# All of p @ w_ple beside the last tile's routing, the last two down products by column halves, and a final gate that begins on the first halves

## The chip, the cores and the metric

One core of a Trainium2 chip runs the whole program. PE is the tensor engine, DVE the vector engine, ACT the scalar engine, POOL and SP mainly issue DMAs here. The metric is the device time of one execution in microseconds; lower is better.

## The reference

One layer on 1024 tokens (rows) of 1024 columns, in float32. After attention and a gated linear mixer the layer ends so:

```python
    h = h + merged @ w_out[l]
    h = h + expert_choice_ffn(rmsnorm(h, norm_ffn[l]), w_router[l],
                              w_exp_gate[l], w_exp_up[l], w_exp_down[l])
    ple_gate = jax.nn.sigmoid(rmsnorm(h, norm_ple[l]) @ w_ple_gate[l])
    h = h + ple_gate * (p[l] @ w_ple[l])
return rmsnorm(h, norm_final)
```

`expert_choice_ffn` has 16 experts. Each takes the 128 tokens with the largest affinity to it, computes `silu(x @ gate) * (x @ up) @ down` with three weights of 1024x1024, scales by the affinity and adds the result to those tokens' rows of h. p has 1024 rows of 256 columns, `w_ple` is 256x1024.

## The kernel before

Rows are worked in eight tiles of 128. To keep float32 precision every product is made of three matmuls (`mm3`): both operands are split into a high part, rounded by ACT (L131, L828, L851), and the rest, which DVE makes (`split`, `parts`, `mpiece`). A product of a tile with a 1024x512 block is thus 24 matmuls of 512 columns.

The part up to h = h + merged @ w_out is followed by the routing. For each tile PE multiplies by `w_out` (`w_half`), DVE adds the old h, ACT and PE make logits (`h_turned`, `router`, `affinities`, `aff_turned`), and DVE sorts the affinities of all tiles (`one_tile` and others). When the last tile (7) is sorted, a threshold per expert is spread by two small transposes of `cg`, ranks come from matmuls with `tri` and `ones`, and `tokens(0)` and `gather(0)` fetch the first expert's rows. Half of p @ w_ple (rows 0 to 511) lies beside this: p is turned on PE (`p_turned`) after tile 5 and multiplied in eight half products of six matmuls (`p_half`), which ACT scales into a buffer `pw` that is stored to the DRAM tensor `pw_d` after each four.

The expert loop runs gate and up of expert e, then down of expert e-1. Weights come in pieces of 1 MB through a ring of 15 buffers (`cycle`) from several pools (wraw, rawA to rawE, rawX), which also hold other things before and after the loop. `hidden_turned` transposes the product of gate and up. Each down product is scaled on ACT into `y` and added to h in DRAM (`h_d`) by an indirect DMA that POOL issues (the scatter).

After the loop the second half of p is loaded, turned and multiplied, the weight `w_pg` (`w_ple_gate`) is loaded and split with its gain, h is read back, and `front(t)` and `ple(t)` make the final gate: transposes of h, a sum of squares (`junk`, ACT), 48 matmuls, then tanh, product with p's rows, sums and the last norm.

While `in_order` is set PE keeps the order of the code; before, it is unset after the last down product. Elsewhere a scheduler orders each engine, and an engine works its queue strictly in order. PSUM has eight banks of 512 columns, in four pairs `mm`, `b`, `tr` (transposes) and `a`.

Of the kernel before, what the change touches and what calls it, by code (L numbers as in the profile page):

```python
# [9 lines left out]
F32 = mybir.dt.float32  # L10
# [11 lines left out]
NT = 8  # L22
D = 1024
KC = 8
# [43 lines left out]
def tile_hybrid_block(  # L68
# [57 lines left out]
    def turn(*args):  # L126
        return on_pe(nc.tensor.transpose(*args))  # L127
# [1003 lines left out]
        elif t == 6:  # L1131
            merged(top[0:NE], one_tile(6), slice(0, NE), top)

    placed = None
    in_order[0] = True
    for t in range(NT):
        was = [{}, {}]
        if t:
            was = [{3: partial(h_turned, t - 1), 6: partial(router, t - 1)},
                   {1: partial(affinities, t - 1), (3 if t > 5 else 7): partial(aff_turned, t - 1)}]  # L1140
        for c in range(2):
            w_half(t, c, was[c])

        if t == 2:
            p_raw = p_load(slot(rawX, (2, 4, 256))[:, 0], 0)
            wp = parts(loaded(rawX, (2, D), w_ple), (2, D), (rawC, rawC))
        if t == 5:
            pT = slot(rawC, (2, 4, 2, 128), F32R)
            p_turned(p_raw, pT)


    def p_half(n):
        nonlocal pw
        i, c = n // 2, n % 2
        if n % 4 == 0:
            pw = slot(rawX, (2, D))
        p_product(pw, pT, wp, i, (c,))
# [5 lines left out]
    for f, more in ((h_turned, (1,)), (router, (2,)), (affinities, (3, 4)), (aff_turned, (5, 6, 7))):  # L1163
        f(NT - 1)
        for n in more:
            p_half(n)
    last = one_tile(NT - 1)
    sO.close()
    eg = ctx.enter_context(pool("eg", bufs=2))
# [8 lines left out]
    pt = bank("a")  # L1178
    for i in range(2):
        turn(pt[:, i * NE:(i + 1) * NE], cg[:, i:i + 1].to_broadcast([NE, 128]), ident[0:NE, 0:NE])  # L1180
    thr = o1.tile([128, 2, NE], F32, name="thr")
    nc.vector.tensor_copy(thr, pt[:, 0:2 * NE].rearrange("p (i e) -> p i e", i=2))

# [24 lines left out]
    def tokens(e):  # L1208
        oh = eg.tile([128, NT, 128], BF16, name="oh", bufs=1)
        nc.vector.tensor_tensor(oh, posT[:, :, e:e + 1].to_broadcast([128, NT, 128]),  # L1210
                                iot.unsqueeze(1).to_broadcast([128, NT, 128]), op=ALU.is_equal)
        pi = bank("a")
        for t in range(NT):
            nc.tensor.matmul(pi[:, 0:2], oh[:, t], tok[:, t], start=t == 0, stop=t == NT - 1)  # L1214
# [10 lines left out]

    found = tokens(0)
    gathered = gather(0)

    so1.close()


# [69 lines left out]
    def up(e, after):  # L1301
# [6 lines left out]
        for c in range(2):  # L1308
            cc = slice(c * 512, c * 512 + 512)
            nc.vector.scalar_tensor_tensor(s["hid"][:, cc], pu[c], s["col"][:, NE:NE + 1], s["hid"][:, cc],  # L1310
                                           op0=ALU.mult, op1=ALU.mult)

    def hidden_turned(e):
        st[e]["hT"] = hl_pair(e2, "hT")
        for g in range(2):
            turned(st[e]["hid"], *st[e]["hT"], g, "tr")

# [29 lines left out]

    begin(0)
    for e in range(NE):
        last = {1: partial(hidden_turned, e)} if e == NE - 1 else {}  # L1350
        gate(e, {1: partial(hidden_turned, e - 1)} if e else {0: first_tokens})
        up(e, {1: partial(tokens_of, e + 2)} if e else {2: partial(ahead, 1)})
        if e:
            down(e - 1, {0: partial(ahead, e + 1), **last})
    down(NE - 1, {})

    in_order[0] = False


    def next_slot(shape, dt=F32):  # L1360
        return slot(next_pool(), shape, dt)

    cycle, n_pieces = [rawC] * 4 + [rawX] * 2 + [wraw] * 2 + [rawE] * 2 + [rawB] * 2 + [rawD], [0]
    pws = {}
    p_raw = p_load(next_slot((2, 4, 256))[:, 0], 4)
    wp = parts(loaded(next_pool(), (2, D), w_ple), (2, D), (next_pool(), next_pool()))
    pT = next_slot((2, 4, 2, 128), F32R)
    p_turned(p_raw, pT)
    wg = {(k, 0): mpiece(w_pg, 4 * k, 0, next_pool(), LL, gain=plcol) for k in range(2)}
    for i in range(4):  # L1370
        if i % 2 == 0:
            pw = next_slot((2, D))
        p_product(pw, pT, wp, i)
        pws[4 + i] = pw[:, i % 2]
    sE.close()
    f2 = ctx.enter_context(pool("f2", bufs=2, side="right"))
    hs_ = {}

    def rows(src, t, n=2):

        r = next_pool().tile([128, 2, D], F32, tag="raw", name="raw")
        return r, nc.sync.dma_start(r[:, 0:n], src[t * 128:(t + n) * 128].rearrange("(c p) n -> p c n", p=128)).ins

    def keep(d, t, n, r):
        d.update({t + i: r[:, i] for i in range(n)})

    r, first = rows(h_d, 0, 1)
    keep(hs_, 0, 1, r)
    with tc.issue_after(first):
        wg.update({(k, 1): mpiece(w_pg, 4 * k, 512, next_pool(), AA, gain=plcol) for k in range(2)})  # L1390
        keep(pws, 0, 2, rows(pw_d, 0)[0])
        keep(hs_, 1, 2, rows(h_d, 1)[0])
        nfin = next_pool().tile([128, 2, D], F32, tag="raw", name="raw")[:, 0]
        nc.sync.dma_start(nfin, bcast_row(norm_final, D))
        for t in (2, 4, 6):
            keep(hs_, t + 1, 2 if t < 6 else 1, rows(h_d, t + 1, 2 if t < 6 else 1)[0])
            if t == 2:
                keep(pws, t, 2, rows(pw_d, t)[0])
    F = {}

    def transposed(src, th, tl, g):

        pt = bank("tr")
        for c in range(4):
            turn(pt[:, c * 128:(c + 1) * 128],
                                src[:, (g * 4 + c) * 128:(g * 4 + c + 1) * 128], ident)
        split(th[:, g * 4:g * 4 + 4], tl[:, g * 4:g * 4 + 4], pt.rearrange("p (c t) -> p c t", c=4))

    def front(t):
        ht = hs_[t]  # L1410
        nT = hl_pair(f2, "nT")
        for g in range(2):
            transposed(ht, *nT, g)
# [6 lines left out]
        F[t] = ht, nT, rh  # L1420

    def ple(t):
        tt = slice(t * 128, (t + 1) * 128)
        ht, nT, rh = F[t]
        pw = pws[t]
        last = t == NT - 1
        groups = [(0, 512), (512, 256), (768, 256)] if last else [(0, 512), (512, 512)]
        ss = small.tile([128, 3], F32, name="ss3")
        for i, (c0, n) in enumerate(groups):
            po = bank("mm")  # L1430
            for k in range(KC):
                w = wg[k // 4, c0 // 512]
                ws = slice(c0 % 512, c0 % 512 + n)
                mm3(po[:, 0:n], nT[0][:, k], nT[1][:, k], w[0][:, k % 4, ws], w[1][:, k % 4, ws], k == 0, k == KC - 1)
# [7 lines left out]
        nc.vector.tensor_reduce(sm, ss[:, 0:len(groups)], axis=X, op=ALU.add)  # L1442
        rs = rstd_of(sm, D)
        for c in range(2):
            cc = slice(c * 512, c * 512 + 512)
            nc.vector.scalar_tensor_tensor(ht[:, cc], ht[:, cc], rs, nfin[:, cc], op0=ALU.mult, op1=ALU.mult)
            (nc.sync if last else nc.gpsimd).dma_start(out[tt, cc], ht[:, cc])

    front(0)
    front(1)  # L1450
    for t in range(NT):
        if t + 2 < NT:
            front(t + 2)
        ple(t)


# [29 lines left out]
```

## Time and profile before

| | |
|---|---|
| three runs | 1714.88, 1716.77, 1717.15 us; median 1716.77 |
| profiled execution: own time | 1719.85 us |
| its span in the profile | 1718.1 us |
| PE busy | 1649.0 us, 96% of the span |
| DVE, ACT busy | 1175.6 us, 903.4 us |
| mean granted PE clock | 0.985 of full speed |

The span is the time from the first to the last record; the execution's own time holds 1.75 us around it. Times in the text count from the start of the span.

### The profile page before, as it was taken

The numbers are of one execution on the slowest core, as the hardware profiler recorded it, in microseconds if no ns is written. First come the engines' busy times: TensorE is split into PE (matmuls) and PEld (weight loads), VectorE is DVE, ScalarE is ACT, GpSimd is POOL, SyncE is SP. The second block draws the span as 40 slices with busy tenths as digits, with TensorE's granted clock in tenths as the row PEclk, the third lists the DMA queues.
The fourth block names the chain that finished last, engine by engine and source line by source line (L and its number), as shares of the span: only waits on it lengthen the run. The fifth ranks groups of instructions, "written<-read, shape, count | busy, mean of one in ns | idle before, by whom it ended". The sixth has DMA issues, their size and how long they took to land. (4 is left out here: it accounts for less than half of the span.)

```text
span 1718.1 us, 23091 instructions
## 1 busy us (share of the span) xinstructions
PE 1649.0 (96%) x8795; PEld 1356.6 (79%) x8795; DVE 1175.6 (68%) x2228; ACT 903.4 (53%) x1265; POOL 155.8 (9%) x186
## 2 busy tenths in 40 slices
PE   6998999999999999999999869999999999999897
PEld 6977766667989898988887647888888887777786
DVE  7546755543474747463356878999999998888566
ACT  4235555441453535352033237777777777777632
POOL 1013300000000000000001110111111111100010
PEclk9999999999999999999999979999999999999999
DMA  6032302325112121126452589999999999992711
GB/s 233 2 106 103 130 26 62 112 85 184 50 55 69 44 80 39 49 74 226 153 197 112 189 328 383 383 395 388 392 397 390 396 387 368 377 379 90 269 50 49
DMA packets 123607, 335.06 MB, mean 195 GB/s; under 512 B 9180, under 2 KB 41988, under 8 KB 123496
## 3 DMA queue, kind: packets, MB, share of 16 engines
q1 hardware_dynamic: 106784, 277.96, 44.2%
q0 software_dynamic: 14704, 53.17, 9.1%
q10 hardware_dynamic: 2008, 2.46, 0.4%
q8 instruction: 69, 1.13, 0.3%
q14 instruction: 42, 0.34, 0.1%
HBM read 290.50 MB, written 43.06 MB: 194 GB/s over the span
## 5 line engine op out<-in xcount | busy, mean ns | idle before, releaser
L131 DVE TENSOR_TENSOR slot<-slot 128x2048 fp32r<-128x2048 f32 (+1 forms) x200 | 446.4, 2245 | 52.7 <-ACT slot L131 50.2
L131 ACT CAST slot<-slot 128x2048 fp32r<-128x2048 f32 (+1 forms) x200 | 374.8, 1879 | 103.9 <-PE ps_mm L124 56.7
L124 PE MATMUL ps_mm<-aT_h,wh 128*128 128x512 f32 x512 | 203.0, 397 | 1.2 <-ACT sgr L273 1.2
L124 PE MATMUL ps_mm<-aT_h,wl 128*128 128x512 f32 x512 | 204.1, 399 | 0.0
L124 PE MATMUL ps_mm<-aT_l,wh 128*128 128x512 f32 x512 | 203.8, 398 | 0.0
L124 PE MATMUL ps_mm<-slot,xt_h 128*128 128x512 f32 x512 | 161.6, 396 | 3.1 <-DVE slot L131 2.7
L124 PE MATMUL ps_b<-slot,xt_h 128*128 128x512 f32 x512 | 160.2, 393 | 4.0 <-DVE slot L131 4.0
L124 PE MATMUL ps_mm<-slot 128*128 128x512 f32 x576 | 142.1, 401 | 0.0
L124 PEld LDWEIGHTS ps_mm<-slot 128*128 128x128 f32 x576 | 108.1, 192 | 24.7 <-issue 1.4
L124 PEld LDWEIGHTS ps_b<-slot,xt_h 128*128 128x128 f32 x512 | 95.1, 188 | 24.8 <-DVE slot L131 5.7
L124 PEld LDWEIGHTS ps_mm<-slot,xt_h 128*128 128x128 f32 x512 | 95.7, 190 | 23.8 <-DVE slot L131 3.5
L124 PEld LDWEIGHTS ps_mm<-aT_h,wh 128*128 128x128 f32 x512 | 97.2, 190 | 18.7 <-ACT sgr L273 1.4
L124 PEld LDWEIGHTS ps_mm<-aT_h,wl 128*128 128x128 f32 x512 | 97.5, 190 | 18.3 <-issue 1.2
L124 PEld LDWEIGHTS ps_mm<-aT_l,wh 128*128 128x128 f32 x512 | 97.1, 190 | 18.3 <-issue 1.2
L131 DVE TENSOR_TENSOR wl<-raw,wh 128x2048 fp32r<-128x2048 f32 (+1 forms) x29 | 61.5, 2121 | 64.1 <-ACT wh L131 64.1
L124 PE MATMUL ps_mm<-slot,xt_l 128*128 128x512 f32 x256 | 100.4, 392 | 0.6 <-DVE xt_l L131 0.6
L131 ACT CAST wh<-raw 128x2048 fp32r<-128x2048 f32 (+1 forms) x30 | 52.1, 1735 | 92.0 <-PE ps_mm L124 87.3
L124 PE MATMUL ps_b<-slot,xt_l 128*128 128x512 f32 x256 | 99.8, 390 | 0.0
L124 PE MATMUL ps_mm<-wh,aT_l 128*128 128x256 f32 x320 | 89.4, 280 | 1.8 <-DVE aT_l L131 1.8
L124 PE MATMUL ps_mm<-wh,aT_h 128*128 128x256 f32 x320 | 90.7, 283 | 0.4 <-DVE sgr L615 0.4
L124 PE MATMUL ps_mm<-wl,aT_h 128*128 128x256 f32 x320 | 89.6, 280 | 0.0
L124 PE MATMUL ps_mm<-slot,nT_h 128*128 128x512 f32 (+1 forms) x272 | 81.8, 381 | 0.3 <-ACT nT_h L131 0.3
(381 smaller groups left out, 3311.4 us busy)
## 6 DMA issues: line engine op xcount, KB each, us to landing
slot<-in_w_exp_gate_dram SPq DMA_DIRECT2D x64, 1024.0 KB, 7.9
slot<-in_w_exp_down_dram SPq DMA_DIRECT2D x64, 1024.0 KB, 8.3
slot<-in_w_exp_up_dram SPq DMA_DIRECT2D x60, 1024.0 KB, 7.7
raw<-in_w_in_dram SPq DMA_DIRECT2D x16, 1024.0 KB, 6.6
raw<-in_w_in_dram SPq DMA_DIRECT2D x14, 512.0 KB, 5.2
sg_d<-sgr POOLq DMA_DIRECT2D x14, 512.0 KB, 3.0
xn_d<-xa POOLq DMA_DIRECT2D x8, 520.5 KB, 3.8
xt<-in_x_dram SPq DMA_DIRECT2D x8, 512.0 KB, 6.7
```

What stands on the lines that cost most here:

```text
L124: return on_pe(nc.tensor.matmul(*args, **kw))
L131: return nc.scalar.copy(hi, src), eng.tensor_sub(lo, src, hi)
```

## The change

1. p is loaded whole after tile 2 and turned in two parts, after tiles 4 and 5. Half products 8 to 11 stand after the first eight, 12 behind the transposes of `cg`, 13 and 14 behind the rank matmuls, 15 behind `gather(0)`. The search of the first expert's tokens takes its place in PE's fixed order. Nothing of p is left after the expert loop but the reading of `pw_d`.
2. The down products of experts 14 and 15 go in column halves, in the order 14 first half, 15 first half, 14 second half, 15 second half, each with a scatter of 128x512 into h seen as 2048 rows of 512. Expert 15's hidden rows are turned behind the first piece.
3. The first halves of rows 0 to 255 of h are read between the second and the third scatter, and turned inside and behind the last half product. The gate's first 4 of 8 blocks of k of tiles 0 and 1 (48 matmuls) stand ahead of everything that needs the second halves. PE's order stays fixed to the end.

```diff
@@ -1142,11 +1142,13 @@
         if t == 2:
-            p_raw = p_load(slot(rawX, (2, 4, 256))[:, 0], 0)
+            p_raw = slot(rawX, (2, 4, 256))
+            for i in range(2):
+                p_load(p_raw[:, i], 4 * i)
...
-        if t == 5:
-            pT = slot(rawC, (2, 4, 2, 128), F32R)
-            p_turned(p_raw, pT)
+        if t in (4, 5):
+            pTs.append(slot(rawC, (2, 4, 2, 128), F32R))
+            p_turned(p_raw[:, t - 4], pTs[-1])
...
+    for n in range(8, 12):
+        p_half(n)
     last = one_tile(NT - 1)
...
+    p_half(12)
...
+    p_half(13)
+    p_half(14)
...
     gathered = gather(0)
-
+    p_half(15)
     so1.close()
...
+    def down_half(e, c, po, after=()):
+
+        s = st[e]
+        cc = slice(c * 512, c * 512 + 512)
+        for k2 in range(2):
+            n = n_pieces[0]
+            raw = loaded(next_pool(), (4, 512), w_ed[e][k2 * 512:k2 * 512 + 512, cc])
+            hi, lo = [slot(rawE if n % 3 == 2 else whl, (4, 512), F32R) for _ in range(2)]
+            split(hi, lo, raw)
+            for k in range(4):
+                kk = 4 * k2 + k
+                mm3(po, s["hT"][0][:, kk], s["hT"][1][:, kk], hi[:, k], lo[:, k], kk == 0, kk == KC - 1)
+            for f in after if k2 == 0 else ():
+                f()
+        nc.scalar.mul(s["y"][:, cc], po, s["col"][:, e:e + 1])
+        nc.gpsimd.indirect_dma_start(out=h_d[:, :].rearrange("t (c n) -> (t c) n", c=2), in_=s["y"][:, cc],
+                                     in_offset=None, compute_op=ALU.add,
+                                     out_offset=bass.IndirectOffsetOnAxis(ap=idx2[:, e % 2, c:c + 1], axis=0))
...
-    down(NE - 1, {})
-
-    in_order[0] = False
...
+    down_half(e0, 0, po[0], (partial(hidden_turned, e1), first_rows))
+    down_half(e1, 0, po[2])
+    r01 = rows(rawD, h_d, 0, LO, queue=nc.gpsimd)
+    hs_.update({0: r01[:, 0], 1: r01[:, 1]})
+    cycle = [rawX] * 2 + [wraw] * 2
+    down_half(e0, 1, po[1])
...
+    down_half(e1, 1, po[3], (partial(first_turn, 0),))
+    first_turn(1)
...
+    begun = {}
+    for t in range(2):
+        begun[t] = [bank("b" if t else "mm") for _ in range(2)]
+        for po, (c0, n) in zip(begun[t], columns(t)):
+            product(po, t, c0, n, range(4))
     front(0)
     front(1)
```

How instructions move. On PE in the routing, before (-) and after (+); `affA` is the transpose of tile 7's affinities, `cg` the threshold, `tri` the rank matmuls:

```order
-L124 MATMUL ps_b<-slot 128x512 x18
+L124 MATMUL ps_b<-slot 128x512 x42
 L127 MATMUL ps_a<-ident,cg 128x16 x2
+L124 MATMUL ps_b<-slot 128x512 x6
 L124 LDWEIGHTS tri
 L124 MATMUL ps_a<-msk,tri 128x256
```

24 matmuls of p now stand between the affinities and the threshold, six between it and the ranks.

On POOL at the end of the expert loop, after the change (L1335 is the scatter of a half, from y for expert 14 and from a buffer named hid for 15, L1392 the read of h, DMASW and DMAHW are DMA semaphores):

```order
L1335 DMA h_d<-y,idx_14170 2048x512 [waits DMASW6_49,Activation_49]
L1335 DMA h_d<-hid,idx_14170 2048x512 [waits DMASW7_49,DVE_49,Activation_49]
L1392 DMA raw<-h_d 128x2x512 [waits DMAHW3_49,DMAHW4_49,DMAHW2_49,DMAHW5_49,DMAHW1_49,DMAHW6_49,DMAHW0_49,DMAHW7_49,DMASW0_49,DVE_49]
L1335 DMA h_d<-y,idx_14170 2048x512 [waits DMASW1_49,Activation_49]
L1335 DMA h_d<-hid,idx_14170 2048x512 [waits DMASW2_49,Activation_49]
```

Where there were two scatters of whole rows there are four of half rows and a read between them, and each waits for the DMA ahead of it.

On PE and then on ACT, after the change, where the gate's first halves end (`ps_b<-slot x24` is tile 1's part of them; the transposes are those of the second halves of tiles 0 and 1, then both halves of tile 2):

```order
L124 MATMUL ps_b<-slot 128x512 x24
L127 MATMUL ps_tr<-ident,raw 128x128 [waits DMAHW5_49,PE_49]
L127 MATMUL ps_tr<-ident,raw 128x128 x3
L127 MATMUL ps_tr<-ident,raw 128x128 [waits PE_49]
L127 MATMUL ps_tr<-ident,raw 128x128 x3
L127 MATMUL ps_tr<-ident,raw 128x128 [waits DMAHW6_49,DVE_49]
L127 MATMUL ps_tr<-ident,raw 128x128 x3
L127 MATMUL ps_tr<-ident,raw 128x128 [waits DVE_49]
L127 MATMUL ps_tr<-ident,raw 128x128 x3
L124 MATMUL ps_mm<-slot 128x512 [waits Activation_49]
```

```order
L1457 ACTIVATE junk,ssf<-raw 128x1024 [waits DMAHW5_49,DMASW1_49]
L1457 ACTIVATE junk,ssf<-raw 128x1024 [waits Activation_49]
L1457 ACTIVATE junk,ssf<-raw 128x1024 [waits DMAHW6_49,Activation_49]
L1457 ACTIVATE junk,ssf<-raw 128x1024 [waits DVE_49,Activation_49]
L131 CAST slot<-ps_tr 128x512 [waits PE_49] x2
L131 CAST nT_h<-ps_tr 128x512 [waits PE_49] x2
```

ACT's queue has the sums of squares of tiles 0 to 3 ahead of the casts of the second halves, and the third of them waits for the same load (DMAHW6) as PE's transposes of tile 2.

## Rows read from the trace of the kernel before

**Rows 1.** The page, part 1: busy us, share of the span, instructions.
```profile
PE 1649.0 (96%) x8795; PEld 1356.6 (79%) x8795; DVE 1175.6 (68%) x2228; ACT 903.4 (53%) x1265; POOL 155.8 (9%) x186
```

**Rows 2.** Windows of 20 us: length, PE, PEld, DVE, ACT, POOL busy, PEclk, DMA, GB/s.
```profile
1000.00:1020.00 20.00, 6.01 (x43) 4.57 (x41) 14.87 (x57) 7.67 (x9) 4.08 (x4) 0.69 0.76 294
...
1600.00:1620.00 20.00, 16.05 (x62) 12.30 (x61) 11.79 (x27) 15.04 (x26) 0.00 (x0) 0.83 0.89 331
```

**Rows 3.** The chain that ended last, in order of time, within the final gate.
```profile
1642.17 10.69 PE ps_mm L124 x47
```

**Rows 4.** Timeline of PE, tail: start, us, engine line op out<-in xcount [idle before <-releaser].
```profile
1569.23 0.61 PE L124 MATMUL ps_mm<-slot,hT_h 128*128 128x512 f32 x2
...
1594.19 1.03 PE L127 MATMUL ps_tr<-ident,slot 128*128 128x128 f32 x8
...
1606.12 6.96 PE L124 MATMUL ps_b<-slot 128*128 128x512 f32 x18 [3.33 <-ACT slot L1042]
...
1614.30 0.73 PE L124 MATMUL ps_mm<-slot,nT_h 128*128 128x512 f32 x2 [0.34 <-ACT nT_h L131]
...
1640.87 0.64 PE L127 MATMUL ps_tr<-ident,raw 128*128 128x128 f32 x4
...
1708.79 0.28 PE L124 MATMUL ps_mm<-slot,nT_l 128*128 128x256 f32 x1
```

**Rows 5.** A window of 1 us inside the wait for p's products.
```profile
1605.00:1606.00 1.00, 0.00 (x0) 0.00 (x0) 1.00 (x3) 1.00 (x3) 0.00 (x0) 0.50 0.85 319
```

**Rows 6.** Timeline of POOL and SP: the last scatter, the first read of h.
```profile
1595.35 1.54 POOL L1328 DMA_INDIRECT h_d<-y,idxs  x1 [9.85 <-ACT y L1327]
...
1601.63 0.34 SPq L1382 DMA_DIRECT2D raw<-h_d  x1
```

**Rows 7.** DMA issues, single ones and groups: KB each, median us to landing.
```profile
h_d<-y,idxs POOLq DMA_INDIRECT x1, 9.5
h_d<-y,idxs POOLq DMA_INDIRECT x1, 6.1
raw<-h_d SPq DMA_DIRECT2D x1, 512.0 KB, 3.6
h_d<-ht POOLq DMA_DIRECT2D x8, 512.0 KB, 2.9
xg<-xn_d,idxs POOLq DMA_INDIRECT x1, 6.2
xg<-xn_d,idxs POOLq DMA_INDIRECT x16, 8.7
```

**Rows 8.** Timeline of ACT and DVE in the tail.
```profile
1593.70 1.37 ACT L1327 ACTIVATE y<-ps_b,col 128x512 f32<-128x512 f32 x2 [3.70 <-PE ps_b L124]
...
1613.66 1.08 ACT L131 CAST nT_h<-ps_tr 128x512 fp32r<-128x512 f32 x2
...
1614.58 1.28 DVE L131 TENSOR_TENSOR nT_l<-ps_tr,nT_h 128x512 fp32r<-128x512 f32 x2
...
1629.41 1.08 ACT L1416 ACTIVATE junk<-raw 128x1024 bf16<-128x1024 f32 x1
...
1630.62 1.06 ACT L1416 ACTIVATE junk<-raw 128x1024 bf16<-128x1024 f32 x1
```

**Rows 9.** Timeline of PE behind tile 4's products.
```profile
945.83 0.92 PE L127 MATMUL ps_tr<-ident,ht 128*128 128x128 f32 x4 [2.67 <-DVE ht L1063]
```

**Rows 10.** Timeline of PE in the routing of the last tile.
```profile
1011.79 0.37 PE L124 MATMUL ps_a<-msk,tri 128*128 128x256 bf16 x1 [0.90 <-DVE msk L1187]
...
1015.42 0.38 PE L1214 MATMUL ps_a<-tok,oh 128*128 128x2 bf16 x8 [2.50 <-DVE oh L1210]
1022.68 1.94 PE L127 MATMUL ps_a<-ident,xg 128*128 128x128 f32 x8 [6.89 <-DMA xg<-xn_d,idxs]
```

**Rows 11.** A window of 2 us as the first gather is issued.
```profile
1016.00:1018.00 2.00, 0.00 (x0) 0.00 (x0) 2.00 (x2) 0.00 (x0) 1.66 (x1) 0.50 0.00 0
```

**Rows 12.** Timeline of ACT's DMA queue: the second store of pw.
```profile
1005.01 0.39 ACTq L1159 DMA_DIRECT2D pw_d<-slot  x1
```

More of the change, by code (lines that the diff above doesn't have):

```diff
@@ L1132, in aff_turned @@
             merged(top[0:NE], one_tile(6), slice(0, NE), top)
-    placed = None
+    placed, pTs = None, []
     in_order[0] = True
@@ L1156, in p_half @@
             pw = slot(rawX, (2, D))
-        p_product(pw, pT, wp, i, (c,))
+        p_product(pw, pTs[i // 4], wp, i % 4, (c,))
         if n % 4 == 3:
@@ L1213, in tokens @@
         for t in range(NT):
-            nc.tensor.matmul(pi[:, 0:2], oh[:, t], tok[:, t], start=t == 0, stop=t == NT - 1)
+            (nc.tensor.matmul if e else matmul)(pi[:, 0:2], oh[:, t], tok[:, t], start=t == 0, stop=t == NT - 1)
         idx = idxs[:, e:e + 1]
@@ L1311, in up @@
                                            op0=ALU.mult, op1=ALU.mult)
+    def down_half(e, c, po, after=()):
[15 more added lines that the diff above has]
+                                     out_offset=bass.IndirectOffsetOnAxis(ap=idx2[:, e % 2, c:c + 1], axis=0))
     def hidden_turned(e):
-        st[e]["hT"] = hl_pair(e2, "hT")
+        st[e]["hT"] = hl_pair(e2, "hT" if e < NE - 1 else "xt")
         for g in range(2):
@@ L1349, in tile_hybrid_block @@
     for e in range(NE):
-        last = {1: partial(hidden_turned, e)} if e == NE - 1 else {}
         gate(e, {1: partial(hidden_turned, e - 1)} if e else {0: first_tokens})
         up(e, {1: partial(tokens_of, e + 2)} if e else {2: partial(ahead, 1)})
-        if e:
-            down(e - 1, {0: partial(ahead, e + 1), **last})
-    down(NE - 1, {})
-    in_order[0] = False
-    def next_slot(shape, dt=F32):
-        return slot(next_pool(), shape, dt)
-    cycle, n_pieces = [rawC] * 4 + [rawX] * 2 + [wraw] * 2 + [rawE] * 2 + [rawB] * 2 + [rawD], [0]
@@ L1364, in tile_hybrid_block @@
[L1364 to L1374, printed above, removed]
+        if 0 < e < NE - 1:
+            down(e - 1, {0: partial(ahead, e + 1)})
@@ new lines, in turned_half, with rows @@
+    def turned_half(ht, nT, g):
+        pt = bank("tr")
+        for c in range(4):
+            turn(pt[:, c * 128:(c + 1) * 128], ht[:, (g * 4 + c) * 128:(g * 4 + c + 1) * 128], ident)
+        split(nT[0][:, g * 4:g * 4 + 4], nT[1][:, g * 4:g * 4 + 4], pt.rearrange("p (c t) -> p c t", c=4))
+    def rows(rp, src, t, cc=slice(None), r=None, queue=nc.sync):
+        r = rp.tile([128, 2, D], F32, tag="raw", name="raw") if r is None else r
+        queue.dma_start(r[:, :, cc], src[t * 128:(t + 2) * 128, cc].rearrange("(c p) n -> p c n", p=128))
+        return r
@@ new lines, in tile_hybrid_block, with first_rows @@
+    e0, e1 = NE - 2, NE - 1
+    po = two_banks() + two_banks()
+    idx2 = eg.tile([128, 2, 2], I32, name="idx2", bufs=1)
+    for e in (e0, e1):
+        for c in range(2):
+            nc.vector.tensor_scalar(idx2[:, e % 2, c:c + 1], st[e]["idx"], 2.0, float(c), op0=ALU.mult, op1=ALU.add)
+    for e, name in ((e0, "y"), (e1, "hid")):
+        st[e]["y"] = e2.tile([128, D], F32, name=name) if e == e0 else None
+    LO, HI = slice(0, 512), slice(512, D)
+    hs_, nTs = {}, {}
+    def first_rows():
+        st[e1]["y"] = e2.tile([128, D], F32, name="hid")
@@ L1375, in tile_hybrid_block, with first_turn @@
+    down_half(e0, 0, po[0], (partial(hidden_turned, e1), first_rows))
[4 more added lines that the diff above has]
+    down_half(e0, 1, po[1])
+    def first_turn(t):
+        nT = slot(whl, (2, KC, 128), F32R)
+        nTs[t] = nT[:, 0], nT[:, 1]
+        turned_half(hs_[t], nTs[t], 0)
+    down_half(e1, 1, po[3], (partial(first_turn, 0),))
+    first_turn(1)
     sE.close()
     f2 = ctx.enter_context(pool("f2", bufs=2, side="right"))
-    hs_ = {}
@@ L1379, in rows @@
[L1379 to L1398, printed above, removed]
@@ L1399, in tile_hybrid_block @@
-    F = {}
[L1401 to L1407, printed above, removed]
+    wg = {}
+    for k in range(2):
+        for c in range(2):
+            pl = AA if c else (wraw if k else rawB,) * 2
+            wg[k, c] = mpiece(w_pg, 4 * k, 512 * c, rawX if k else rawC, pl, gain=plcol)
@@ new lines, in tile_hybrid_block @@
+    pws = {}
+    for t in (0, 2):
+        r = rows(rawX, pw_d, t)
+        pws.update({t: r[:, 0], t + 1: r[:, 1]})
+        if t == 0:
+            rows(rawD, h_d, 0, HI, r01)
+    for t in (2, 4, 6):
+        r = rows(rawC, h_d, t)
+        hs_.update({t: r[:, 0], t + 1: r[:, 1]})
+        if t == 2:
+            nfin = slot(rawC, (2, D))[:, 0]
+            nc.sync.dma_start(nfin, bcast_row(norm_final, D))
+        else:
+            r = rows(rawE, pw_d, t)
+            pws.update({t: r[:, 0], t + 1: r[:, 1]})
@@ L1409, in front @@
+    F = {}
     def front(t):
         ht = hs_[t]
-        nT = hl_pair(f2, "nT")
-        for g in range(2):
-            transposed(ht, *nT, g)
+        if t not in nTs:
+            nTs[t] = hl_pair(f2, "nT")
+            turned_half(ht, nTs[t], 0)
+        turned_half(ht, nTs[t], 1)
         junk = f2.tile([128, D], BF16, name="junk", bufs=1)
@@ L1419, in front, with columns, product, ple @@
         nc.vector.tensor_scalar(rh, rs, 0.5, None, op0=ALU.mult)
-        F[t] = ht, nT, rh
-    def ple(t):
+        F[t] = rh
+    def columns(t):
+        return [(0, 512), (512, 256), (768, 256)] if t == NT - 1 else [(0, 512), (512, 512)]
+    def product(po, t, c0, n, ks):
+        for k in ks:
+            w = wg[k // 4, c0 // 512]
+            ws = slice(c0 % 512, c0 % 512 + n)
+            mm3(po[:, 0:n], nTs[t][0][:, k], nTs[t][1][:, k], w[0][:, k % 4, ws], w[1][:, k % 4, ws],
+                k == 0, k == KC - 1)
+    def ple(t, begun=None):
         tt = slice(t * 128, (t + 1) * 128)
-        ht, nT, rh = F[t]
-        pw = pws[t]
+        ht, rh, pw = hs_[t], F[t], pws[t]
         last = t == NT - 1
-        groups = [(0, 512), (512, 256), (768, 256)] if last else [(0, 512), (512, 512)]
         ss = small.tile([128, 3], F32, name="ss3")
[L1429 to L1434, printed above, removed]
+        for i, (c0, n) in enumerate(columns(t)):
+            po = begun[i] if begun else bank("b" if t % 2 else "mm")
+            product(po, t, c0, n, range(4 if begun else 0, KC))
             cc = slice(c0, c0 + n)
@@ L1441, in ple @@
         sm = small.tile([128, 1], F32, name="ssm")
-        nc.vector.tensor_reduce(sm, ss[:, 0:len(groups)], axis=X, op=ALU.add)
+        nc.vector.tensor_reduce(sm, ss[:, 0:len(columns(t))], axis=X, op=ALU.add)
         rs = rstd_of(sm, D)
@@ L1453, in tile_hybrid_block @@
             front(t + 2)
-        ple(t)
+        ple(t, begun.get(t))
 _INS = ['x', 'p', 'positions', 'norm_mix', 'w_in', 'gla_gate_up_fwd', 'gla_gate_bias_fwd',
```

## The prediction

> **What bounds the kernel now.** The page comes first: the tensor engine (PE) is busy for 1649.0 of 1718.1 us [rows 1], so moving work pays only where PE idles or runs slow. The windows of 20 us say where that is: 1000 to 1020 (6.01 us busy, the routing of the last tile) and 1600 to 1620 (16.05 busy at a clock of 0.83) [rows 2]. The chain of waits gives the pace of the final gate: 47 matmuls of 512 columns in 10.69 us, 0.227 each [rows 3]. PE's timeline of the tail is then read row by row [rows 4]: the down product of expert 14 begins at 1569.23; the last down product hands over to the transposes of p at 1594.19; 18 products of p take 6.96 us from 1606.12, 0.387 each, after a wait of 3.33; the final gate's first matmul is at 1614.30; the fifth tile's transposes begin at 1640.87; the last matmul ends at 1709.07. The slow products have a granted clock of 0.50, the 1.2 GHz level [rows 5]: the idle time before them cost 18 x (0.387 - 0.227) = 2.9 us more. The span ends 9.0 us after PE, in the last row sums and stores, which stay as they are.
>
> So 1614.30 - 1594.19 = 20.1 us of the tail hold p, its slow clock and a wait for h. That is the most that the change can win there. What matters is what PE waits for instead.
>
> **The tail, step by step, in the clock of the old trace.** PE order after the change: eight pieces of 12 matmuls (2.73 us each), the eight transposes of expert 15's hidden rows behind the first piece (0.8), four transposes of tile 0 behind the seventh, four of tile 1 behind the eighth, 48 gate matmuls on the first halves, then transposes of the second halves. From 1569.2 the pieces end at 1571.9, 1575.5, 1578.2, 1580.9, 1583.7, 1586.4 and 1589.1, where PE must have the first-half rows of h.
>
> (a) The first wait. POOL's order makes a chain: scatter of expert 14's first half, of 15's, read of rows 0 to 255, and only then the second halves. A full scatter was issued 0.28 us after y and let the read of h go 6.3 us after its start [rows 6]; it landed after 6.1 us when little else moved and after 9.5 beside about 3 MB of loads [rows 7]. No row shows a half one. Bounds: 4.1 us (1.5 on POOL as before, and of the rest, some 4.6 us, a little over half), and 9.5. I take 5.6, near the full one's 6.1, because the POOL time and the landing don't shrink and two loads of w_ple_gate fall beside it. y(14) is ready at 1576.4 and the scatter lands at 1582.3; y(15), one product (0.7 [rows 8]) after 1581.2, is ready by then, so its scatter runs 1582.6 to 1588.2; the read takes 2.9 (512 KB from POOL [rows 7]) and a small issue gap: 1591.3. PE, ready at 1589.1, waits 2.2 us. Idle of 2.67 us at 945.83 did cost clock [rows 9], so I add 0.7. Eighth piece and transposes: 1595.7. Gate matmuls on the first halves, 48 x 0.227 = 10.9: 1606.6.
>
> The Trainium skill, "DMA: Bandwidth & Descriptors", section "Anatomy of one DMA", speaks against cutting transfers up: a DMA pays about 2 us whatever its size plus its bytes at 436 GB/s. By it a half scatter, 256 KB less, would take 6.1 - 0.6 = 5.5 us, an estimate from that page; the tail would then end about 0.3 us earlier than with 5.6. No row here shows a half scatter, so the trace can't yet decide.
>
> (b) The second wait. Scatter of 14's second half: 1591.5 to 1597.1; 15's (y at 1596.1): 1597.4 to 1603.0; read of the second halves of rows 0 to 255, 3.6 us for 512 KB [rows 7]: 1606.8; rows 256 to 511, 1 MB behind it at about 390 GB/s, 2.7 us: 1609.5. PE transposes tiles 0 and 1 by 1607.6. Next in its order are tile 2's transposes, which need a transposing bank back, and the bank waits for ACT. ACT has four sums of squares ahead of that cast, 1.21 us from start to start, the last two for tiles 2 and 3 [rows 8]: two from 1606.8, two from 1609.5, until 1612.0. Cast (0.5) and VectorE's difference (0.7) [rows 8] free the bank at 1613.3, the second bank at 1614.0. The gate goes on at 1614.4: PE idles 5.7 us, longer than the 3.33 of [rows 4] that cost 2.9, so I add 2.9.
>
> (c) The rest. Left are 24 matmuls (5.45), eight transposes (0.8), 24 matmuls (5.45) and what ran from 1640.87 to 1709.07 (68.2): 79.9. 1614.4 + 79.9 + 2.9 + 9.0 = 1706.2 against 1718.1: **11.9 us won**. The splitting of the gate's weights hides behind the pieces and the 10.9 us; if that cover were gone, each of its 16 blocks of 128x512 would cost about a cast and a difference of that shape, 1.2 [rows 8].
>
> **The routing.** Added to PE there: eight transposes and two splits in tile 4's turn, and eight half products, 48 matmuls. (d) PE waits there anyway for VectorE, 2.67 us [rows 9], so the 0.8 of transposes hide, but the two differences go onto VectorE, which is that wait: 1.3 us [rows 8]; bounds 0 and 2.1. (e) Four halves stand ahead of the threshold transposes, where PE idled anyway. One stands before the rank matmuls, which waited 0.90, two before the token search, which waited 2.50 [rows 10]. With 1.36 us a half and ACT's drain between them, 1.1 us of delay is left; nothing if they fit, 4 at the 1.2 GHz clock. (f) The last half hides in the 6.89 us wait for the gather [rows 10]. But the loads of gate(1) wait in the new order for that last half, as they use the buffers of w_ple and p; they start as the gather fetches. DMA stood at 0.00 then [rows 11]. The gather landed in 6.2 us, and in 8.7 as the median of 16, most of them beside loads [rows 7]: between 0 and 2.5, I take 1.2. Sum: 1.3 + 1.1 + 1.2 = **3.6 lost**, between 0 and 8.6. The experts between start later and are otherwise the same; the ring of 15 buffers is refilled later, but gate(1) is used some 25 us after its loads begin.
>
> **Sum.** 11.9 - 3.6 = 8.3 us: span 1709.8, own time 1719.85 - 8.3 = 1711.5. The median shown, 1716.77, lies 3.1 below that execution's own time; the forecast for it is 1716.77 - 8.3 = **1708.5 us**.
>
> **The rivals.** *All of the tail is won.* If a half scatter took half of 6.1 us, rows would be there at 1588.3, and 15's second half at 1596.5, its reads at 1600.1 and 1602.8, ACT's sums done at 1605.2, the gate on again at 1607.0 with no clock lost: 1695.9, 22.2 won less 3.6, 1698.2 us. For it: the data part of a scatter is more than half of its time. Against it: the fixed parts.
>
> *The chain of DMAs eats it.* With 9.5 us for the loaded scatter of 15's first half and 6.1 for the others PE waits 6.1 us at tile 0 and loses 2.9 of clock there, the gate goes on at about 1619.7 and the span is 1711.6 + 3.6: 3 us won, 1713.8 us, no measurable change. For it: the 9.5 was measured beside just such loads.
>
> *The routing pays more than the tail wins: slower.* Half product 8 writes a buffer whose 1 MB store of pw must have landed, and half 12 one whose store was issued at 1005.01 [rows 12]. Those products stand in PE's fixed order ahead of the threshold and of the token search. Below a landing at about 1008 and 1012 nothing happens; from there each us counts once. If both stores landed 6 to 7 us later than that, the routing would lose 3.6 + 13 = 16.6 us and the kernel 4.7: 1721.5. Against it: two of the loads that filled the queues there now start only later.
>
> *It does not do what it says:* as the experts are bound by PE, a later start passes through whole, so a delay of 12 us or so in (d) to (f) from many causes would cancel it: 1716.8.
>
> **Chances.** Forecast 0.58, all won 0.17, chain 0.13, slower 0.08, cancelled 0.04. A measurement here tells about 0.2% (3.4 us) from no change: faster 0.75, within 0.2% 0.17, slower 0.08. The forecast's own bounds (scatter 4.1 to 6.1, routing 0 to 8.6) give 1700 to 1714; with the cases beside it 8 in 10 lie between 1698 and 1716.
>
> **What would show it.** A half scatter's issue to landing near 5.6; PE's wait before tile 0's first transposes near 2 us; PE idle near 6 us before the second half of tile 0's gate, released by VectorE behind ACT's sums; PE free of p after the last down product; the gather's first transposes 2 to 5 us later than 1022.68; nothing new between 1060 and 1560. I am wrong if the two waits in the tail are missing or double, or if a store of pw holds PE before the threshold.

## The result, and the profile after

The change made the kernel slower: 1731.15 us median against 1716.96 (six executions each; the ratio leaves out one disturbed execution of the changed kernel, without which its median is 1730.34), a ratio of 1.0069 with a 95% interval of 1.0051 to 1.0086, some 12 us. Forecast was 1708.5. The profiled execution took 1724.22 us with a span of 1722.5; it was the shortest of its kernel.

The page, part 1 (answers to [rows 1]), and from part 4 the chain that ended last, by engine; the last line is that chain in the page of before:

```profile
PE 1647.4 (96%) x8795; PEld 1355.3 (79%) x8795; DVE 1173.9 (68%) x2231; ACT 902.4 (52%) x1264; POOL 159.5 (9%) x189
...
PE 35%; DMA 3%; issue 2%; DVE 1%; ACT 1%; DVEq 0%; ACTq 0%; POOLq 0%
...
PE 37%; DVE 2%; ACT 1%; issue 1%; DMA 0%; DVEq 0%; ACTq 0%; POOLq 0%
```

PE does the same work in a longer span, and transfers now have 3% of the chain where they had 0%. Windows of 20 us (answers to [rows 2]; columns as there):

```profile
1000.00:1020.00 20.00, 16.18 (x88) 11.87 (x86) 13.30 (x55) 11.82 (x15) 2.27 (x1) 1.00 0.74 277
1580.00:1600.00 20.00, 13.55 (x60) 10.89 (x58) 12.48 (x7) 10.72 (x9) 4.98 (x3) 0.89 0.57 157
1600.00:1620.00 20.00, 18.08 (x76) 14.79 (x76) 12.03 (x25) 12.76 (x22) 3.16 (x2) 0.85 0.49 129
1620.00:1640.00 20.00, 16.25 (x70) 13.62 (x71) 13.16 (x56) 10.95 (x22) 0.00 (x0) 0.83 0.81 320
1660.00:1680.00 20.00, 17.58 (x82) 13.77 (x80) 10.87 (x35) 6.26 (x14) 1.12 (x3) 1.00 0.14 52
```

The window of the routing is filled as intended, 16.18 us busy for 6.01. But in the tail PE idles in three places where before it had one long wait: 1580 to 1600, 1620 to 1640, and again among the last tiles (1660 to 1680), which ran without a gap before.

To see where the span grew it is cut at three rows that both kernels have: the turn of tile 3's logits, ahead of which the change only adds one load of 512 KB of p, issued at 836; the first gather's transposes; and the first product of down(14). PE's timeline, before:

```profile
935.48 0.27 PE L127 MATMUL ps_a<-ident,lg 128*128 128x128 f32 x1
```

PE's timeline, after (answers to [rows 10] and [rows 4]):

```profile
932.55 0.27 PE L127 MATMUL ps_a<-ident,lg 128*128 128x128 f32 x1
...
1008.75 3.03 PE L124 MATMUL ps_b<-slot 128*128 128x512 f32 x12 [1.93 <-ACT slot L1042]
1011.71 0.28 PE L127 MATMUL ps_a<-ident,cg 16*128 16x16 f32 x2
...
1016.83 0.35 PE L124 MATMUL ps_a<-tok,oh 128*128 128x2 bf16 x8
...
1029.52 1.94 PE L127 MATMUL ps_a<-ident,xg 128*128 128x128 f32 x8 [10.84 <-DMA xg<-xn_d,idxs]
...
1573.42 0.62 PE L124 MATMUL ps_mm<-slot,hT_h 128*128 128x512 f32 x2
...
1600.68 1.09 PE L127 MATMUL ps_tr<-ident,raw 128*128 128x128 f32 x4 [7.13 <-DMA raw<-h_d]
...
1623.75 1.97 PE L127 MATMUL ps_tr<-ident,raw 128*128 128x128 f32 x8 [4.99 <-DVE slot L131]
1625.38 7.82 PE L124 MATMUL ps_mm<-slot 128*128 128x512 f32 x24
...
1652.50 1.32 PE L127 MATMUL ps_tr<-ident,raw 128*128 128x128 f32 x8 [1.18 <-DVE nT_l L131]
...
1713.31 0.28 PE L124 MATMUL ps_b<-slot,nT_l 128*128 128x256 f32 x1
```

The stretches are differences of those rows and of the span's end; the third column is a second profiled execution of the changed kernel (first run below):

| us | before | after | after, again |
|---|---|---|---|
| to tile 3's logits | 935.48 | 932.55 | 935.02 |
| routing, to the first gather's transposes | 87.20 | 96.97 | 99.37 |
| experts, to down(14) | 546.55 | 543.90 | 545.11 |
| tail, to the end | 148.87 | 149.08 | 149.00 |
| span | 1718.1 | 1722.5 | 1728.5 |

Two things are read from it. The first profile flattered the change by 2.9 us in the first stretch; 2.5 of them lie between two executions of the same kernel (932.55 and 935.02), so they are chance. And the routing lost 9.8 to 12.2 us where 3.6 were forecast, while the tail, which should have won 11.9, won nothing.

The chain that ended last shows why, step by step from the first half scatter to the gate's second half:

```profile
1580.96 5.66 DMA h_d<-y,idx
1586.69 0.48 issue
1587.38 8.40 DMA h_d<-hid,idx
1595.81 0.53 issue
1596.34 4.21 DMA raw<-h_d
1600.59 0.69 issue
1601.29 4.92 DMA h_d<-y,idx
1606.24 1.61 issue
1607.87 0.19 issue
1608.06 5.00 DMA h_d<-hid,idx
1613.07 4.16 DMA raw<-h_d
1617.32 1.16 ACT junk L1457 x2
...
1623.10 0.61 DVE slot L131
1623.75 1.97 PE ps_tr L127 x8
```

Six transfers in a row and not one matmul: from 1581 to 1617 PE's work merely lies beside the chain. The half scatters with nothing else moving (52 to 57 GB/s in all) took 4.92 to 5.66 us, the one beside two loads of w_ple_gate (266 GB/s) 8.40. The estimate of 5.5 us worked out from the Trainium skill, "DMA: Bandwidth & Descriptors", section "Anatomy of one DMA", lies among the first kind and far from the second.

### The profile page after: what moved, and what is told of

Its sections match the earlier page's. It is cut to its first block, busy times and chain, and to the rows that moved or that the text cites. A ratio compares the mean times of both kernels' runs of the same rounds, so it can differ in the third digit from the quotient of the medians.

```text
span 1722.5 us, 23109 instructions
## 1 busy us (share of the span) xinstructions
PE 1647.4 (96%) x8795; PEld 1355.3 (79%) x8795; DVE 1173.9 (68%) x2231; ACT 902.4 (52%) x1264; POOL 159.5 (9%) x189
## 5 line engine op out<-in xcount | busy, mean ns | idle before, releaser
L124 PE MATMUL ps_b<-slot,xt_h 128*128 128x512 f32 x544 | 171.5, 396 | 3.2 <-DVE slot L131 3.2
L124 PE MATMUL ps_mm<-slot 128*128 128x512 f32 x624 | 155.0, 403 | 0.0
L124 PEld LDWEIGHTS ps_mm<-slot 128*128 128x128 f32 x624 | 117.8, 193 | 26.7 <-issue 1.4
L124 PEld LDWEIGHTS ps_b<-slot,xt_h 128*128 128x128 f32 x544 | 102.1, 190 | 25.1 <-DVE slot L131 4.5
L124 PE MATMUL ps_b<-slot,xt_l 128*128 128x512 f32 x272 | 106.8, 393 | 0.0
L131 DVE TENSOR_TENSOR wl<-raw,wh 128x2048 fp32r<-128x2048 f32 (+1 forms) x29 | 61.5, 2121 | 64.3 <-ACT wh L131 64.3
L124 PE MATMUL ps_b<-slot 128*128 128x512 f32 x336 | 80.9, 393 | 2.5 <-ACT slot L1042 2.5
```

Source lines behind the costliest of these rows:

```text
L124: return on_pe(nc.tensor.matmul(*args, **kw))
L131: return nc.scalar.copy(hi, src), eng.tensor_sub(lo, src, hi)
```

## The experiments

Two theories stood against each other. **Several prices:** the gather beside loads, the halves ahead of the threshold, the loaded scatter, ACT's queue and the fixed order of PE each cost their own few us, and can be taken out one by one. **Chance and one wait:** what the first profile shows beyond the forecast belongs to that one execution, and the waits of the tail share one cause, so that removing one only moves it. Each kernel was timed beside the kernel before. e1 to e4, e5 to e8, e9 to e12 and e13 ran on four chips, so medians are compared within a group and ratios across groups. The stretches are those of the table above, from one profiled execution of each.

| run | median us | ratio to before, 95% | routing | gather lands after | tail |
|---|---|---|---|---|---|
| e1 changed kernel again | 1728.27 | 1.0062, 1.0046 to 1.0078 | 99.4 | 11.8 | 149.0 |
| e2 p moved, old tail | 1720.28 | 1.0023, 1.0014 to 1.0032 | 97.6 | 11.9 | 142.2 |
| e3 new tail, half of p left out | 1718.31 | 1.0010, 1.0001 to 1.0019 | 84.6 | 6.1 | 148.4 |
| e4 old tail, half of p left out | 1710.96 | 0.9968, 0.9956 to 0.9980 | 87.5 | 6.2 | 141.3 |
| e5 last half behind the gather | 1726.94 | 1.0051, 1.0034 to 1.0068 | 91.7 | 6.3 | 147.3 |
| e6 gate's order free | 1721.93 | 1.0026, 1.0015 to 1.0038 | 99.3 | 11.8 | 142.8 |
| e7 gate's loads behind rows | 1729.38 | 1.0064, 1.0048 to 1.0080 | 97.0 | 11.9 | 150.8 |
| e8 sums behind casts | 1722.02 | 1.0027, 1.0017 to 1.0038 | 99.9 | 11.7 | 144.4 |
| e9 read ahead of gate's loads | 1722.78 | 1.0037, 1.0025 to 1.0050 | 97.4 | 11.7 | 144.8 |
| e10 six halves in the gather's wait, old tail | 1715.26 | 0.9992, 0.9982 to 1.0001 | 94.5 | 6.1 | 141.9 |
| e11 e5, e6 and e8 together | 1714.62 | 0.9989, 0.9979 to 1.0000 | 94.5 | 6.4 | 137.0 |
| e12 e6 and e8, halves as in e10 | 1709.51 | 0.9962, 0.9947 to 0.9976 | 92.9 | 6.1 | 136.9 |
| e13 e12 and e9 | 1710.55 | 0.9958, 0.9944 to 0.9972 | 96.6 | 6.2 | 136.2 |

How far stretches of the same code spread can be read from the table: the routing of the change took 97.0 to 99.9 us in seven profiles, the old one 84.6 to 87.5 in three, and the tail of the change 147.3 to 149.1 in three.

**Which part loses (e1 to e4).** e1 is the changed kernel without an edit.

> The changed kernel once more, for a second profile: its timed runs lay between 1724 and 1733 us, and the one with a profile was the fastest. Theory (fixed prices): the same three places cost as in the first profile, the gather lands 11 to 12 us after its issue, PE waits 7 us for the first rows and 5 us for the second ones, time 1724 to 1733. Rival (chance of one execution): the gather lands within 7 us or the wait for the first rows is under 4 us this time, and the time lies apart from the first by as much.

The gather landed after 11.8 us again, PE waited 7.5 us for the first rows and 1.5 and 5.3 for the second ones. So the waits are no chance of one execution, and that half of the rival falls; whether the waits of the tail share a cause is still open here (e13).

e2 has the routing of the change (the diff's part up to `p_half(15)`) and the old tail, whose p is read back:

```
-    p_raw = p_load(next_slot((2, 4, 256))[:, 0], 4)
...
-        p_product(pw, pT, wp, i)
-        pws[4 + i] = pw[:, i % 2]
...
-            if t == 2:
-                keep(pws, t, 2, rows(pw_d, t)[0])
+            keep(pws, t, 2, rows(pw_d, t)[0])
```

> Only the first part: all of p in the routing, and the tail as before without its p (the rows of pw are read back). Without p the old tail should start its gate when h has come, about 1607.5 instead of 1614.3, so p was worth some 7 us there. Theory (the routing pays 6.8 us, most of it the gather beside the loads): about 1717 us, no change to before. Rival (the routing pays 3.6 us as forecast, the rest of the 6.8 was chance): about 1713.5 us.

e3 is the changed kernel with the routing part of the diff undone, and `rows(rawE, pw_d, t % 4)`:

> The routing as before with half of p only; the tail of the change. The p of the last four tiles is left out: their gate takes the rows of the first four. Theory: the routing is back at 1024.4 for the first matmul of expert 0, gather 6 to 7 us, and the time is that of the changed kernel less 6.8, about 1724 us by its median; the tail itself wins nothing over the old one. Rival: only 3.6 us come back, about 1727.5 us.

e4 is the kernel before with the edit of e2 in the tail alone, and `t % 4` in its read:

> The routing and the tail as before, with the second half of p left out of the tail: the last four tiles take the rows of the first four. What p cost in the old tail is read from it: theory 7 us (about 1710 us), since PE must wait for the scatter and the read of h anyway until about 1606. Rival: all 20 us between the last down product and the first gate product go, about 1697 us. The difference of this one to the run with p moved is the price of p in the routing, and to the run with the new tail the price of the halved tail.

The four kernels without and with each part add up. From e4, p in the routing costs 1720.28 - 1710.96 = 9.3 us, the halved tail 1718.31 - 1710.96 = 7.4, and both together would make 1727.6; the changed kernel measured 1728.27 on that chip. Two expectations missed by this: e2 was expected at 1717 and e3 at 1724 us, since the price of p in the routing had been put at 6.8. What p cost in the old tail is the third number: 1716.58 - 1710.96 = 5.6 us (3.4 to 7.6 by the interval, 7.5 by the tails of the two profiles), not the 20.1 that its products spanned there. PE's timeline of e4 says why:

```profile
1604.83 1.94 PE L127 MATMUL ps_tr<-ident,raw 128*128 128x128 f32 x8 [10.70 <-DMA raw<-h_d]
1606.59 1.22 PE L124 MATMUL ps_mm<-slot,nT_h 128*128 128x512 f32 x2
```

With no p, PE idles 10.70 us for the scatter and the read of h. In the old tail p's products were the cover of that wait. So the change moves p to where it costs 9.3 us, to win 5.6 to 7.5.

**The gather (e5).** The last half product goes behind `begin(0)`, which holds the gather's transposes:

```
     gathered = gather(0)
-    p_half(15)
...
     begin(0)
+    p_half(15)
```

> The changed kernel with the last half product of p put behind the first gather's transposes, so that the loads of gate(1), which wait for that half, can't start while the gather fetches. Theory (the gather lands 11.7 us after its issue because those loads run beside it): 6 to 7.5 us from issue to landing, PE's wait for it near 7 us, one half product of 1.4 us given back behind it, so about 4 us off the changed kernel's 1728 to 1731. Rival (the stores of pw or the loads of up on the same queue hold it): the landing stays above 10 us and the time goes up by the half product.

POOL's row of the gather and ACT's row of the last store of pw in the changed kernel, then PE's timeline of e5:

```profile
1017.73 2.83 POOL L1229 DMA_INDIRECT xg<-xn_d,idxs  x1 [18.02 <-DVE idxs L1223]
...
1019.94 0.37 ACTq L1161 DMA_DIRECT2D pw_d<-slot  x1
```

```profile
1018.20 0.35 PE L124 MATMUL ps_a<-tok,oh 128*128 128x2 bf16 x8
1025.50 1.94 PE L127 MATMUL ps_a<-ident,xg 128*128 128x128 f32 x8 [6.95 <-DMA xg<-xn_d,idxs]
```

6.3 us to the landing instead of 11.7. In the changed kernel two loads of gate(1) were issued between 1018.48 and 1019.36, while POOL's row of the gather runs from 1017.73 to 1020.56, and a store of pw at 1019.94; in e5 those loads come at 1029.22 and the store at 1030.09. The two loads of up behind the gather on POOL's queue are issued in both, so they are not it. Loads and store moved together; which of them weighs more this run can't say (in e12 a store issued at 1020.92 and a load of down at 1021.29, in the gather's last 1.2 us, left it at 6.1). From the token search to the gather's transposes it is 7.3 us as before ([rows 10]: 1022.68 - 1015.42), where the changed kernel had 12.7. Of the 5.4 won the experts' stretch gives 3.7 back (547.6 instead of 543.9): the half product now stands on the path and takes 2.3 us there, most of it at a granted clock of 0.50, and PE's waits in the stretch are 8.2 us instead of 6.3. So the run shows what delays the gather, but its time, 1.0051 against 1.0062 for e1, is not clear of the noise.

**The tail's waits (e6 to e9).** e6 frees PE's order for the final gate:

```
+    in_order[0] = False
     begun = {}
```

> The changed kernel with PE's order left to the scheduler from the final gate on, as it was before the change. Theory (the fixed order puts the transposes of tile t+2 straight behind those whose casts wait for tile t's last product): the three waits of 1.18 us in the tiles behind the fourth go, the transposes stand inside the products, 3.5 us less. Rival (the waits come with the transposing banks, whatever the order): they stay, no change.

The three waits of 1.18 us are gone, and the tail is 6.3 us shorter, where 3.5 were expected. The rest can be read from PE's rows: one of those tiles takes 13.4 us in the changed kernel and 11.9 in e6, as the transposes behind each wait are slower too, 4.7 in three tiles; and from the end of the second wait to the first matmul of tile 2's products it is 16.4 and 15.0. PE's waits from 1585 to the end, after and e6 (engine, line <- releaser: us in total, times, longest):

```profile
PE ps_tr L127 <- DMA raw<-h_d: 7.1, 1, 7.1
PE ps_tr L127 <- DVE slot L131: 5.0, 1, 5.0
PE ps_tr L127 <- DVE nT_l L131: 3.5, 3, 1.2
```

```profile
PE ps_tr L127 <- DMA raw<-h_d: 7.2, 1, 7.2
PE ps_mm L124 <- ACT slot L131: 4.8, 1, 4.8
```

e7 was to hold two loads behind the read of h:

```
-            wg[k, c] = mpiece(w_pg, 4 * k, 512 * c, rawX if k else rawC, pl, gain=plcol)
+            with tc.issue_after(r01_in) if k else ExitStack():
+                wg[k, c] = mpiece(w_pg, 4 * k, 512 * c, rawX if k else rawC, pl, gain=plcol)
```

> The changed kernel with two of the four loads of w_ple_gate held until the read of rows 0 to 255 is issued; they ran beside the scatter of expert 15's first half. Theory (that scatter's 9 us came from the loads): it lands in 5 to 6 us as the one ahead of it did, PE's wait before tile 0 falls from 7.1 to about 4 us and the clock loses less, some 3.5 us off the changed kernel. Rival (a second scatter behind the first is slow by itself): still 8 to 9 us, no change, or worse where the loads then delay the gate.

It does not test its theory: the read was on POOL's queue and the loads on SP's, where they were issued as in e1, and the scatter took 8.83 us beside them. Its tail, 1.7 us longer, is within the spread. e9 keeps that edit, for the loads, and puts the read on SP's queue, ahead of three of the loads:

```
-    r01 = rows(rawD, h_d, 0, LO, queue=nc.gpsimd)
+    r01 = rows(rawD, h_d, 0, LO)
```

> What the run before meant to try and did not do (its two loads were still issued beside the scatter): the read of rows 0 to 255 now goes through SP's queue, and three of the four loads of w_ple_gate stand behind it there, so they can't be issued before the scatter of expert 15's first half has landed. Theory (the 8.4 to 8.8 us of that scatter come from the loads): it lands 5 to 6 us after its issue, PE's wait before tile 0 falls from 7.1 to 4 us. What the time does depends on the loads, which now come later. Rival (the second of two scatters is slow by itself): 8 us and more again.

The chain of e9:

```profile
1594.62 4.75 DMA h_d<-hid,idx
1599.38 3.99 DMA raw<-h_d
1603.51 1.09 PE ps_tr L127 x4
```

The same second scatter takes 4.75 us when nothing moves beside it, for 8.40, and PE's wait falls from 7.13 to 2.83. So it was the loads, not the place in the chain; the third scatter, which the three held loads now run beside, took 8.4 us in e9 instead of 4.92, and PE waits 2.63 us for the second halves' rows.

e8 puts each sum of squares behind its tile's cast:

```
-        turned_half(ht, nTs[t], 1)
+        cast = turned_half(ht, nTs[t], 1)
...
-        nc.scalar.activation(junk, ht, AF.Square, accum_out=ss)
+        with tc.issue_after(cast):
+            nc.scalar.activation(junk, ht, AF.Square, accum_out=ss)
```

> The changed kernel with each tile's sum of squares on ACT issued behind that tile's second cast, where four sums stood ahead of the first two casts. Theory (the second wait is ACT's queue): PE's wait of 5.0 us falls to 1 to 2 us, about 3.5 us off the changed kernel, more if the clock does not fall. Rival (the wait is for the rows of tile 2, 1 MB behind the others): PE still waits 4 to 5 us, now released by a read of h.

PE's timeline of e8 where the changed kernel waited 4.99 us:

```profile
1627.38 0.63 PE L127 MATMUL ps_tr<-ident,raw 128*128 128x128 f32 x4 [1.60 <-DVE rs_t L147]
1628.27 0.74 PE L127 MATMUL ps_tr<-ident,raw 128*128 128x128 f32 x4 [0.26 <-DVE slot L131]
```

1.86 us are left, so most of the second wait was ACT's queue, and the tail is 4.7 us shorter. With PE's order free as well (e11) it is gone: 0.24 us.

**A version that wins (e10 to e13).** e10 takes e2 and places the products otherwise; its edit is also that of e12 and e13:

```
-    for n in range(8, 12):
+    for n in range(8, 10):
         p_half(n)
...
-    p_half(12)
...
-    p_half(13)
-    p_half(14)
...
-    p_half(15)
+    for n in range(10, 16):
+        p_half(n)
```

> The old tail without its p, as in the second run, and p's products otherwise placed in the routing: two halves ahead of the threshold transposes, the last six behind the first gather, where PE waits for it anyway. Theory: six halves take 8.2 us and the gather 7, so PE is held 1 to 2 us there; the gather lands in 6 to 7 us, as its loads wait for the last half; the threshold is no more delayed. About 9.3 us of the routing's price shrink to 3 or 4: 1714 to 1715 us. Rival (the late start of gate(1)'s loads is paid in expert 1): a stall at gate(1) of several us and 1717 to 1720 us.

> The changed kernel with three of the single changes together: last half behind the gather's transposes, PE's order free in the final gate, sums behind the casts. Theory (three separate prices): 4 + 3.5 to 7 + 3.5 to 7 us less than 1728 to 1731, so 1712 to 1719 us. Rival (they share one wait): not under 1720 us.

> The changed kernel with PE's order free in the final gate, the sums behind the casts and the last six half products of p in the wait for the gather. Theory: as the run with three repairs and 2 to 4 us less, since the threshold is not delayed: 1710 to 1715 us, faster than both kernels. Rival: no less than that run, if the six halves hold PE as long as they no longer delay the threshold.

All three came out close to what the several prices say; e10 and e11 only reach the time of the kernel before. e12 beats the kernel before by 7 us (0.4%), and the changed kernel by 17 to 19 (by ratios and by medians of different chips). PE's timeline of e12:

```profile
1009.82 0.25 PE L127 MATMUL ps_a<-ident,cg 16*128 16x16 f32 x1 [2.50 <-DVE cg L1179]
...
1015.09 0.37 PE L124 MATMUL ps_a<-tok,oh 128*128 128x2 bf16 x8 [2.49 <-DVE oh L1214]
...
1025.56 1.04 PE L127 MATMUL ps_a<-ident,xg 128*128 128x128 f32 x8
...
1595.93 1.09 PE L127 MATMUL ps_tr<-ident,raw 128*128 128x128 f32 x4 [7.06 <-DMA raw<-h_d]
...
1612.70 1.06 PE L127 MATMUL ps_tr<-ident,raw 128*128 128x128 f32 x8 [0.25 <-DMA raw<-h_d]
```

PE waits for the threshold again (2.50), so nothing of p delays it, and comes to the gather's transposes without a wait. They start 10.5 us behind the token search, where the wait for the gather alone took 7.3 in the kernel before, so the six halves still cost some 3 us there.

> The best run so far (last six halves in the gather's wait, order free, sums behind casts) with the read of rows 0 to 255 on SP ahead of three loads of w_ple_gate. Theory (the wait for the first rows is a price of its own, 4.3 us of idle time and the clock behind it): 4 to 6 us less than that run's 1709.5, about 1705 us. Rival (the rows of tile 0's second half and the late loads are next, as that run's PE waits for both within 0.3 us): no change, 1708 to 1711 us, the idle time stands behind the first gate products.

PE's timeline of e13:

```profile
1597.78 0.63 PE L127 MATMUL ps_tr<-ident,raw 128*128 128x128 f32 x4 [2.83 <-DMA raw<-h_d]
...
1616.69 1.64 PE L127 MATMUL ps_tr<-ident,raw 128*128 128x128 f32 x8 [4.15 <-DMA raw<-h_d]
```

The rival held here: the wait before tile 0 fell from 7.06 to 2.83, but PE then waited 4.15 us instead of 0.25 for the second halves' rows. The three late loads push those back, as the third scatter took 8.5 us beside them; the tail is 136.2 for 136.9. With the other repairs in, the loaded scatter is no price of its own any more.

## Why the prediction was wrong

Three steps failed: the wait for the first rows was priced at 2.2 us and was 7.13, as the scatter beside loads was given the time of an unloaded one (a); the rest of the tail was taken over unchanged though PE's order was now fixed, 5.3 us (c); and the gather beside gate(1)'s loads was priced at 1.2 us and cost 5.4 (f). The halves ahead of the threshold (e) were mis-sized as well.

**What bounds the kernel: the ceiling was not split.** The 20.1 us between the last down product and the gate were called the most that could be won, which they are; but how much of them was work and how much cover was not asked. e4 shows that 5.6 to 7.5 us were p's own. The rest was the wait for h, which any tail has to hide by other means.

**(a) The first wait: the mechanism right, the size wrong.** The chain of scatter, scatter, read was as written, and PE was ready at 1593.5, as forecast for this execution (1589.1 and the 4.2 us by which it began later). Forecast was a wait of 2.2 us; it was 7.13. The terms: the loaded scatter 8.40 and its issue gap instead of 5.6 (3.4 us), the read 4.2 instead of 2.9 (1.3), the first scatter with its gap 6.4 instead of 5.9 (0.5). The 2.9 was the row of a write, `h_d<-ht`; the row of a read of that size in [rows 7] had 3.6. The row for a loaded scatter, 9.5 in [rows 7], stood there, and I took the unloaded 6.1 as nearest although I had counted two loads beside it. That was the rival of the DMA chain, which had 0.13. The clock then cost more too: the eighth piece with its eight transposes took 6.0 us (1600.68 to 1606.72) where 3.5 is its time at the full clock: the granted clock was 0.50 from 1600.68 to 1605, and 2.5 were lost for 0.7.

**(b) The second wait: right.** Forecast 5.7, measured 4.99, with the cause that was named, four sums of squares ahead of the casts; e8 shows it for all but 1.86. ACT's rows after:

```profile
1617.32 1.06 ACT L1457 ACTIVATE junk<-raw 128x1024 bf16<-128x1024 f32 x1 [2.83 <-DMA raw<-h_d]
...
1622.12 1.05 ACT L131 CAST slot<-ps_tr 128x512 fp32r<-128x512 f32 x2
```

**(c) The rest: a step left out.** From 1640.87 on everything was taken over unchanged. But PE's order is now fixed to the end: the transposes of tile t+3 need the banks of those of tile t+2, whose casts, as they write buffers that tile t's products still read, can't start before tile t's last product. ACT's cast at 1651.13 waits for PE, and PE then 1.18 us, in each of three tiles; the whole stretch from 1625.38 to the end was 97.1 instead of 91.8. It could have been read in the new order. e6 shows it.

So the tail lost, against the forecast, 5.2 us before tile 0, 1.8 by the clock behind it and 5.3 at the end: 12.3, as much as the 11.9 that were to be won. In e11 the tail is 137.0, and the 11.9 against before are there after all; but that is luck, since the sum is another one: a first wait of 6.90 and no second one.

**(d) Tile 4 and behind: a little low.** From tile 3's to tile 7's logits the routing took 63.4 and 64.1 us for 61.2 (996.70 - 935.48): 2.2 to 2.9 lost, for 1.3 and a bound of 2.1. The size is uncertain, as the old order took 58.6 and 61.5 in e3 and e4; the twelve profiles with the new one lie between 63.4 and 66.8.

**(e) Halves ahead of the threshold: mis-sized.** From tile 7's logits to the transposes of cg it was 15.75 and 17.39 us (1011.71 - 995.96; 1016.49 - 999.10) for 13.38: 2.4 to 4.0 lost, where 1.1 was forecast for all halves. A part of it is the third rival in small, and the sign that was named for it, a store of pw that holds PE ahead of the threshold: ACT's scaling of half 8 waited 2.07 us for a store to land, and PE 1.93 for ACT. ACT's row after:

```profile
1008.10 1.09 ACT L1042 ACTIVATE slot<-ps_b 128x512 f32<-128x512 f32 x2 [2.07 <-DMA pw_d<-slot]
```

The rival's sum of 16.6 us was far off. e12, with two halves there, has no such loss: 13.37.

**(f) The gather: the largest miss of the routing.** 5.4 us instead of 1.2, twice the upper bound of 2.5, which came from a median of 16 gathers, most of them beside loads. The collision was named, but priced by gathers with other company. Here the loads of gate(1) were issued before POOL had finished issuing the gather. e5 shows that the loss goes with them and the store of pw; which of the two it is stays open.

**Not foreseen, in the other direction:** the experts' stretch became 1.4 to 2.7 us shorter after the later start. The waits of PE there fell from 7.7 us to 6.3; what the rest is stays open.

Forecast for the routing was 3.6, measured 9.8 to 12.2; for the tail -11.9, measured 0.2; for the experts 0, measured -1.4 to -2.7. The sum is 7.3 to 10.9 us by profiles, 11.7 to 14.2 by the medians. The rest lies in the spread of the first stretch and in before's profile, which was 3 us above its median.

## What to carry to other kernels

Before work is moved out of a stretch, ask what waits run under it: what is won is the stretch less the longest chain that it covered, and that can be measured by leaving the work out. Price each transfer of a new chain by the row that has the same company, not by the one of the same size. Loads that have time can be held until the transfer on which the path waits has landed, as for the gather; but look at what they run beside then, since for the scatter of the first rows that only moved the wait (e13). Work that may lie anywhere in a wait belongs behind the last instruction that others wait for, not ahead of it.

## What the hardware showed

The gather and the scatter suffer from company: the gather of 128 rows took 6.1 to 6.4 us with loads of up behind it on its own queue, and 11.7 to 11.9 where two more loads of 1 MB and a store came in beside it; a half scatter took 4.7 to 6.2 alone and 7.9 to 8.8 beside two or three loads, in the second place of the chain or in the third. Between one landing and the next transfer of the chain lay 0.56 to 0.76 us on POOL's queue in the changed kernel (once 1.86), and 0.02 where the read stood on SP's (1613.05 to 1613.07). And one profiled execution of the changed kernel was 2.5 us shorter than the next in the first stretch, so that single profiles are to be compared stretch by stretch.
